# Joins of softmax statistics behind a given product's splits, layer-end tiles in a fixed order, the recurrence's Ln and Exp grouped and its large products off POOL

## The chip, the cores and the metric

The kernel runs on one core of one Trainium2 chip. The metric is the device time of one execution in microseconds (us), the median of several executions. A core has five engines that run side by side and meet only through semaphores: PE (TensorE, matrix products), DVE (VectorE), ACT (ScalarE, functions from tables), POOL (GpSimd) and SP (SyncE), which here issues almost all transfers. Each engine takes its own instructions in the order in which they were written for it.

## The reference, cut to what matters

The reference is two layers of one kind and two of another, on one sequence of 512 tokens with 1024 features. The first block is

```python
for layer in range(2):
    h = rms_norm(x, norm_mix_pre[layer])
    h = dilated_attention_mixer(h, ...) if layer % 2 == 0 else rglru_mixer(h, ...)
    x = x + rms_norm(h, norm_mix_post[layer])
    h = conv_ffn(rms_norm(x, norm_ffn_pre[layer]), ...)
    x = x + rms_norm(h, norm_ffn_post[layer])
```

The attention has eight heads of width 128 and two groups, one on neighbouring tokens and one on every fourth token. Each group gives an output and a log-sum, and the two are joined by a softmax over the groups:

```python
mx = jnp.max(logits, axis=-1, keepdims=True); p = jnp.exp(logits - mx)
s = jnp.sum(p, axis=-1, keepdims=True)
o = jnp.einsum('...qk,...kd->...qd', p, v) / s;  lse = mx + jnp.log(s)
alpha = jax.nn.softmax(jnp.stack(lses), axis=0)
o = jnp.sum(alpha[..., None] * jnp.stack(outs), axis=0)
```

The recurrence of the second layer (LRU) is `h[t] = a[t] h[t-1] + b[t]` with `a = exp(log_a)` and `b = sqrt(1 - a^2) * i * xb`, its output multiplied by `gelu(gate)` and by a weight matrix. `conv_ffn` is an up product, a short causal convolution, `gelu(g) * v` and a down product. The second block (two layers of three attentions with gates and a merge) isn't touched by the change in its own code, but it uses `normed`, which is.

## The kernel before, in words

**Products.** Every product is taken in three matmuls of hi and lo parts (`mm3`, L40 to L47): hi by hi, hi by lo, lo by hi. A weight unit (`wunit`) is loaded by SP into a `ws` buffer of 512 KB, ACT makes its hi part `wh` (L195), DVE, or POOL where it is asked to, the lo part `wl` (L196). `split` does the same for activations. `fms` runs a product with the features as rows, `tm` with tokens as rows: four tiles of 128 tokens by 512 columns each, kept in four PSUM banks, where `tail` says how many of the last steps are done tile by tile, so that the tiles end one after another.

**Order.** The program is written out, and then a scheduler with a simulated timeline sets the order on each engine. Three things bind it: the data, `keep_in_program_order`, which pins an instruction behind everything that was written for its engine before it, and `tc.issue_after`, which sets it behind a given instruction.

**The attention** (`DilatedHead`, `dilated_attention`). Each head has three qkv products for each of two groups and, for every second head, the values. `scores` takes two orders of tokens (order 1 is the strided one), makes min and sum per row (the buffer `W`, by the accumulators of L99 on DVE and L101 on ACT), writes the probabilities into `PA` and `PB`, and sends its half of `W` to DRAM (`dx`, L102) and the other order's half back (`W` from `dx`, L103), since the two orders lay the tokens out differently. `normalize` waits for `W`, joins the statistics (L113 to L120: min, difference, Exp on ACT, product, sum, reciprocal, product, all on the small tile `c`), and scales `PA` and `PB` on POOL (L124, eight instructions). `values` transposes `PA` on PE (L134), splits into `ptA`, multiplies with the values into the only `pv` bank (L45 to L47), copies into `oT`; then the same with `PB` (L145, `ptB`, L153 and L154), where DVE adds two halves into `oT` (L157) and so frees the bank. `NORMALIZE_AFTER` and `VALUES_AFTER` say behind how many of the next head's products `normalize` and `values` are written. L113 is pinned by `keep_in_program_order`.

**The layer's end** (`post_and_next`, `advance`, `normed`, `turned`). The mixer's last product `tm` gives token tiles in two column halves (`y0`, `y1`); each is squared and multiplied by a gain, its reciprocal root-mean-square is made (`rstd2`, a small power on POOL, L347), x is updated (L396), the next norm taken (`normed`, L302 to L309: two squares of 512 columns on ACT, `rstd2`, then one column half on DVE, L309, and the other on ACT and POOL, L306 and L307) and the tile turned on PE (L317).

**The recurrence** (`lru_layer`). `front` does the input product, the convolution (L571, L573) and the gates (L713); `recur` takes four of eight feature tiles at a time: Exp, Tanh, a clamp (L721 to L723), Ln and Exp (L728, L729), then L733 to L740 on DVE but for `y*v`, which is on POOL (L734). The last loop multiplies by the Gelu gate on POOL (L759). The input product's units from the second group of columns on have their lo part made on POOL.

Of the kernel before, what the change touches and what calls it, by code (L numbers as in the profile page):

```python
# [18 lines left out]
D = 1024  # L19
# [11 lines left out]
NORMALIZE_AFTER, VALUES_AFTER = 5, 7  # L31
# [11 lines left out]
def mm3(nc, out, lh, ll, rh, rl, start, stop):  # L43

    nc.tensor.matmul(out, lh, rh, start=start, stop=False)  # L45
    nc.tensor.matmul(out, lh, rl, start=False, stop=False)  # L46
    nc.tensor.matmul(out, ll, rh, start=False, stop=stop)  # L47


class DilatedHead:  # L50
# [54 lines left out]
    def normalize(self):  # L105
# [6 lines left out]

        n.tc.keep_in_program_order(nc.vector.tensor_tensor(r, nm[:, :, 0], nm[:, :, 1], op=OP.min))  # L113
# [46 lines left out]
class Net:  # L160
    def __init__(self, ctx, tc, ins, out):
# [16 lines left out]
        self.junk = self.vp.tile([128, 512], mybir.dt.bfloat16, name="junk")  # L178
# [12 lines left out]
    def split(self, hi, lo, src, eng=None, scale=None):  # L191

        nc = self.nc
        if scale is None:
            nc.scalar.copy(hi, src)  # L195
            (eng or nc.vector).tensor_tensor(lo, src, hi.bitcast(F32), op=OP.subtract)  # L196
        else:
            nc.scalar.mul(hi, src, scale)
            nc.vector.scalar_tensor_tensor(lo, src, scale, hi.bitcast(F32), op0=OP.mult, op1=OP.subtract)

    def wunit(self, src, eng=None):
# [6 lines left out]
        self.split(wh, wl, ws, eng)  # L208
# [6 lines left out]
    def fms(self, w, cols, rh, rl, n=128, kt=KD, group=1, eng=None):  # L215
# [19 lines left out]
    def tm(self, w, col, n, lh, ll, kt=KD, banks=0, tail=0, hold=None):  # L235
# [8 lines left out]
        us = []  # L244
        for k0 in range(0, kt, a):
# [5 lines left out]
            for ks in (ks[:-1], ks[-1:]) if hold and k0 + a == kt else (ks,):  # L251
                if hold and ks[-1] == kt - 1:
                    hold()
                for t in range(NT):
                    for k in ks:
                        mm3(nc, ps[t][:, :n], lh(k, t), ll(k, t), wh[:, k - k0], wl[:, k - k0], k == 0, k == kt - 1)
# [39 lines left out]
    def normed(self, xt, g, xn):  # L296

        nc = self.nc
        ss = self.stat(2)
        halves = (slice(0, 512), slice(512, 1024))  # L300
        for c, cs in enumerate(halves):
            nc.scalar.activation(xn[c], xt[:, cs], AF.Square, accum_out=ss[:, c:c + 1])  # L302
        r = self.rstd2(ss[:, 0:1], ss[:, 1:2])
        for c, cs in enumerate(halves):
            if c:
                nc.scalar.mul(xn[c], xt[:, cs], r)  # L306
                nc.gpsimd.tensor_tensor(xn[c], xn[c], g[:, cs], op=OP.mult)  # L307
            else:
# [1198 lines left out]
```

## Time and profile before

| | us |
|---|---|
| median of 3 executions | 2910.41 (2906.74 to 2910.72) |
| the profiled execution | 2905.02 |
| its span, first to last instruction | 2903.2 |
| PE busy / DVE / ACT / POOL | 2781.5 / 1641.1 / 1302.4 / 666.1 |
| mean granted TensorE clock | 0.983 of full speed |

The profiled execution is one of its own, 5.4 us below the median of the others, and 1.8 us of it lie outside the span. A PE that is busy 96% of the span can be made faster only where it isn't busy, and where it is busy at the lower of its two clocks (1.2 and 2.4 GHz; a granted clock of 0.5 in the records is the lower). In time the attention lies at 13 to 629 us of the span, the first FFN at 629 to 1009, the recurrence at 1009 to 1200, the second FFN at 1200 to 1625, the second block's layers at 1625 to 2275 and 2275 to 2903.

### The profile page before, as it was taken

To read this page: it belongs to the slowest core of one execution; us is meant where nothing else is said; L and a number is where in the kernel's file an instruction comes from. 1 tells how busy PE (TensorE), PEld (TensorE's weight loads), DVE (VectorE), ACT (ScalarE), POOL (GpSimd) and SP (SyncE) were. 2 spreads that over 40 slices of the span, in tenths; PEclk is the share of its full clock that TensorE was granted. 3 is DMA by queue.
4 is the path that set the end of the run, shared out by engine and by line. 5 is a ranking of instruction groups with operands and counts; after the bars stand their busy time and mean duration, and the time that the engine had idled before them with its cause. 6 is when DMAs were issued, how large, how long until landed. Compare 5 with 4: busy or idle time off the path is not lost.

```text
span 2903.2 us, 40547 instructions
## 1 busy us (share of the span) xinstructions
PE 2781.5 (96%) x15005; PEld 2381.3 (82%) x15005; DVE 1641.1 (57%) x3245; ACT 1302.4 (45%) x2570; POOL 666.1 (23%) x771
## 2 busy tenths in 40 slices
PE   8998898889999997999999999999999999999999
PEld 6887777778888885888888898888988898888987
DVE  4235443465552458655533767767654767767653
ACT  3233333354442355444422654665543554665542
POOL 1001110121110125211100343333421343343420
PEclk9999999899999998999999999999999999999999
DMA  5553332243333332433332524113234524113233
GB/s 176 167 159 84 88 97 64 74 130 97 100 107 111 111 122 73 134 99 94 99 127 94 152 69 107 54 50 82 63 88 130 150 66 113 47 50 82 63 98 106
DMA packets 392253, 288.60 MB, mean 99 GB/s; under 512 B 33608, under 2 KB 351816, under 8 KB 392056
## 3 DMA queue, kind: packets, MB, share of 16 engines
q1 hardware_dynamic: 382928, 268.94, 31.8%
q10 hardware_dynamic: 9128, 17.07, 1.6%
q8 instruction: 119, 1.95, 0.3%
q14 instruction: 78, 0.64, 0.1%
HBM read 266.86 MB, written 21.20 MB: 99 GB/s over the span
## 4 chain that ended last, share of the span: by engine, by line
PE 81%; DVE 7%; DMA 5%; issue 3%; ACT 3%; POOL 2%; SPq 0%; DVEq 0%; ACTq 0%; POOLq 0%
PE acc L45 20%; PE acc L46 20%; PE acc L47 20%; PE tr L843 3%; PE pv L903 2%; PE sc L46 2%; PE sc L45 2%; PE sc L47 2%; DMA dx<-W 2%; PE tr L45 1%; DVE wl L196 1%; PE tr L47 1%; PE tr L46 1%; PE pv L47 1%; PE pv L46 1%
## 5 line engine op out<-in xcount | busy, mean ns | idle before, releaser
L196 DVE TENSOR_TENSOR wl<-ws,wh 128x1024 fp32r<-128x1024 f32 (+5 forms) x463 | 550.8, 1190 | 649.5 <-ACT wh L195 645.8
L195 ACT CAST wh<-ws 128x1024 fp32r<-128x1024 f32 (+2 forms) x476 | 469.4, 987 | 754.1 <-PE acc L46 292.0
L45 PE MATMUL acc<-hH,wh 128*128 128x512 f32 (+1 forms) x1928 | 748.0, 389 | 16.9 <-DVE gate L750 8.0
L47 PE MATMUL acc<-hH,wl 128*128 128x512 f32 (+1 forms) x1928 | 744.5, 387 | 2.0 <-POOL wl L196 2.0
L46 PE MATMUL acc<-hL,wh 128*128 128x512 f32 (+1 forms) x1928 | 744.2, 386 | 1.6 <-DVE hL L196 1.4
L45 PEld LDWEIGHTS acc<-hH,wh 128*128 128x128 f32 x1928 | 366.5, 191 | 87.4 <-issue 10.0
L47 PEld LDWEIGHTS acc<-hH,wl 128*128 128x128 f32 x1928 | 367.2, 190 | 72.2 <-POOL wl L196 3.6
L46 PEld LDWEIGHTS acc<-hL,wh 128*128 128x128 f32 x1928 | 367.3, 191 | 69.3 <-DVE hL L196 2.6
L46 PE MATMUL acc<-wl,hH 128*128 128x256 f32 (+3 forms) x928 | 277.4, 300 | 0.9 <-DVE wl L196 0.7
L45 PE MATMUL acc<-wh,hH 128*128 128x256 f32 (+3 forms) x928 | 275.6, 299 | 2.0 <-ACT hH L195 1.5
L47 PE MATMUL acc<-wh,hL 128*128 128x256 f32 (+3 forms) x928 | 274.9, 299 | 0.0
L45 PEld LDWEIGHTS acc<-wh,hH 128*128 128x128 f32 x928 | 177.7, 192 | 8.2 <-ACT hH L195 2.0
L46 PEld LDWEIGHTS acc<-wl,hH 128*128 128x128 f32 x928 | 177.8, 192 | 7.3 <-DVE wl L196 1.8
L47 PEld LDWEIGHTS acc<-wh,hL 128*128 128x128 f32 x928 | 177.7, 192 | 4.3 <-DVE hL L196 0.4
L636 POOL TENSOR_TENSOR cv<-cv 128x512 f32<-128x512 f32 x48 | 62.0, 1291 | 463.0 <-DVE cv L573 449.3
L573 DVE SCALAR_TENSOR_TENSOR cv<-acc,cw,cv 128x511 f32<-128x511 f32 (+1 forms) x192 | 142.5, 746 | 3.2
L124 POOL TENSOR_SCALAR PA<-PA,c 128x256 f32<-128x256 f32 (+1 forms) x32 | 22.0, 704 | 494.2 <-DVE c L120 257.5
L876 ACT ACTIVATE P<-P,soft 128x128 f32<-128x128 f32 (+1 forms) x192 | 108.1, 563 | 60.8 <-DVE soft L875 56.6
L806 POOL TENSOR_TENSOR hst<-hst,mhalf 128x4 f32<-128x4 f32 (+2 forms) x90 | 91.6, 1022 | 175.4 <-DVE hst L805 171.4
L843 PE MATMUL tr<-ident,P 128*128 128x128 f32 x720 | 123.8, 275 | 4.1 <-POOL P L1278 2.2
L875 DVE CUSTOM_DVE_ANT_0 P<-sc,causal 128x128 f32<-128x128 f32 (+1 forms) x192 | 93.1, 485 | 52.7 <-PE tr L843 34.6
L878 POOL TENSOR_SCALAR P<-P,soft,ngate 128x128 f32<-128x128 f32 (+3 forms) x128 | 87.0, 684 | 140.2 <-DVE soft L877 128.8
(464 smaller groups left out, 5159.3 us busy)
## 6 DMA issues: line engine op xcount, KB each, us to landing
ws<-in_w_in_dram SPq DMA_DIRECT2D x116, 512.0 KB
ws<-in_ffn_w_up_dram SPq DMA_DIRECT2D x96, 512.0 KB
ws<-in_attn_w_qkv_dram SPq DMA_DIRECT2D x72, 512.0 KB
ws<-in_ffn_w_down_dram SPq DMA_DIRECT2D x48, 512.0 KB
x<-x ACTq DMA_DIRECT2D x16, 512.0 KB
ws<-in_lru_w_in_dram SPq DMA_DIRECT2D x16, 512.0 KB
ws<-in_w_mem_kv_dram SPq DMA_DIRECT2D x16, 512.0 KB
ws<-in_w_out_dram SPq DMA_DIRECT2D x16, 512.0 KB
```

Source lines behind the costliest of these rows:

```text
L45: nc.tensor.matmul(out, lh, rh, start=start, stop=False)
L46: nc.tensor.matmul(out, lh, rl, start=False, stop=False)
L47: nc.tensor.matmul(out, ll, rh, start=False, stop=stop)
L195: nc.scalar.copy(hi, src)
L196: (eng or nc.vector).tensor_tensor(lo, src, hi.bitcast(F32), op=OP.subtract)
L573: nc.vector.scalar_tensor_tensor(dst[:, s:], ps[:, :T - s], cw(taps - 1 - s), dst[:, s:], op0=OP.mult, op1=OP.add)
L636: nc.gpsimd.tensor_tensor(g, g, v, op=OP.mult)
L806: nc.gpsimd.tensor_tensor(st[:, 1], st[:, 0], self.mhalf[:rows, :nh], op=OP.pow)
L843: self.nc.tensor.transpose(ps[:, a * 128:(a + 1) * 128], s, self.ident)
L875: nc.vector.tensor_tensor_reduce(out=P, in0=S, in1=self.causal[:, 512 - n:512], scale=-1.0, scalar=BIG, op0=OP.add, op1=OP.min, accum_out=m)
L876: nc.scalar.activation(P, P, AF.Exp, bias=m, scale=-1.0, accum_out=s)
L878: nc.gpsimd.tensor_scalar(P, P, r, mult, op0=OP.mult, op1=OP.mult)
```

## The change

Six edits, which need not go together:

1. The attention's min (L113 before, L122 after) is no longer pinned in program order; it is set behind the hi and lo splits of the product that was written just before it (`done`, with `behind`). `VALUES_AFTER` goes from 7 to 6, so `values` follows one product earlier. For the last head, whose joins are made in the out product's `hold`, the joins go behind the last splits of `oT` and of the weight unit.
2. `tm` chains the token tiles of its tail: a tile's tail follows the tile before it, by `issue_after`, and the first tile's tail follows the last matmul ahead of it. After the attention, `y1` as a whole follows the last matmul of `y0`.
3. `normed` takes one square of 1024 columns and one reciprocal root, and makes both column halves on DVE. ACT's product and POOL's product go.
4. In the recurrence, `Ln` of four tiles stands ahead of `Exp` of four tiles by `issue_after`; before, the two were written tile by tile.
5. In the recurrence, `y*v` and `hs*g` go from POOL to DVE.
6. The lo parts of the recurrence's input weights go from POOL to DVE (`eng` is gone from `fms` and `wunit`).

```diff
-NORMALIZE_AFTER, VALUES_AFTER = 5, 7
+NORMALIZE_AFTER, VALUES_AFTER = 5, 6
...
+@contextmanager
+def behind(tc, *ins):
+
+    with ExitStack() as st:
+        for i in ins:
+            if i is not None:
+                st.enter_context(tc.issue_after(i.ins))
+        yield
...
-        n.tc.keep_in_program_order(nc.vector.tensor_tensor(r, nm[:, :, 0], nm[:, :, 1], op=OP.min))
+        nc.vector.tensor_tensor(r, nm[:, :, 0], nm[:, :, 1], op=OP.min)
...
-            us = [self.wunit(wv[:, :, c:c + n], eng if q else None) for c in g]
+            us = [self.wunit(wv[:, :, c:c + n]) for c in g]
...
         for t in range(NT):
-            for k in range(last, kt):
-                wh, wl = us[k // a]
-                mm3(nc, ps[t][:, :n], lh(k, t), ll(k, t), wh[:, k % a], wl[:, k % a], k == 0, k == kt - 1)
+            with behind(self.tc, end):
+                for k in range(last, kt):
+                    wh, wl = us[k // a]
+                    end = mm3(nc, ps[t][:, :n], lh(k, t), ll(k, t), wh[:, k % a], wl[:, k % a], k == 0, k == kt - 1)
+            self.last_pe = end
             yield ps[t]
...
-        ss = self.stat(2)
-        halves = (slice(0, 512), slice(512, 1024))
-        for c, cs in enumerate(halves):
-            nc.scalar.activation(xn[c], xt[:, cs], AF.Square, accum_out=ss[:, c:c + 1])
-        r = self.rstd2(ss[:, 0:1], ss[:, 1:2])
-        for c, cs in enumerate(halves):
-            if c:
-                nc.scalar.mul(xn[c], xt[:, cs], r)
-                nc.gpsimd.tensor_tensor(xn[c], xn[c], g[:, cs], op=OP.mult)
-            else:
-                nc.vector.scalar_tensor_tensor(xn[c], xt[:, cs], r, g[:, cs], op0=OP.mult, op1=OP.mult)
+        ss = self.stat()
+        nc.scalar.activation(xn[2] if len(xn) > 2 else self.junk, xt, AF.Square, accum_out=ss)
+        r = self.rstd(ss, 128, 1.0 / D)
+        for c, cs in enumerate((slice(0, 512), slice(512, 1024))):
+            nc.vector.scalar_tensor_tensor(xn[c], xt[:, cs], r, g[:, cs], op0=OP.mult, op1=OP.mult)
...
-        y1 = self.tm(w, 512, 512, lh, ll, kt=kt, banks=3 if hold else 1, tail=4)
+        y1 = self.tm(w, 512, 512, lh, ll, kt=kt, banks=3 if hold else 1, tail=4, after=self.last_pe if hold else None)
...
+        def normalize(a):
+
+            with behind(self.tc, *done):
+                a.normalize()
...
-                    self.split(v4[:, 0], v4[:, 1], ps, scale=None if u else 128 ** -0.5)
+                    done[:] = self.split(v4[:, 0], v4[:, 1], ps, scale=None if u else 128 ** -0.5)
...
-                last()
+                last((*done, *self.last_split))
...
-        return self.fms(self.i["lru_w_in"][0], self.lru_cols(), *h, group=3, eng=self.nc.gpsimd)
+        return self.fms(self.i["lru_w_in"][0], self.lru_cols(), *h, group=3)
...
-                        nc.scalar.activation(ys[-1], th[2 * m], AF.Ln, bias=tiny)
-                        last = nc.scalar.activation(ys[-1], ys[-1], AF.Exp, scale=-0.5)
+                        last = nc.scalar.activation(ys[-1], th[2 * m], AF.Ln, bias=tiny)
+                with self.tc.issue_after(last.ins):
+                    for y in ys:
+                        last = nc.scalar.activation(y, y, AF.Exp, scale=-0.5)
...
-                    nc.gpsimd.tensor_tensor(y, y, v, op=OP.mult)
+                    nc.vector.tensor_tensor(y, y, v, op=OP.mult)
...
-                nc.gpsimd.tensor_tensor(hs[m], hs[m], g, op=OP.mult)
+                nc.vector.tensor_tensor(hs[m], hs[m], g, op=OP.mult)
```

The change shifts lines: L113 becomes L122, L157 becomes L166, L196 becomes L204, L199 L206, L733 to L740 become L744 to L751, and L750 becomes L761.

On DVE in the attention, at the end of the second head's scores, the order before is this (`ptB` is the lo split of the head before, `c` the joins, `oT` the additions that free the `pv` bank, `wl` and `qk` the splits of the next products):

```order
L196 TENSOR_TENSOR ptB<-tr,ptB 128x512
L113 TENSOR_TENSOR c<-W 128x2x4
L115 TENSOR_TENSOR c<-c,W 128x2x4 x2
L196 TENSOR_TENSOR wl<-ws,wh 128x1024
L157 TENSOR_TENSOR oT<-oT,pv 128x2x128
L199 SCALAR_TENSOR_TENSOR qk<-acc,qk 128x512
L117 TENSOR_TENSOR c<-c,W 128x4x4
L157 TENSOR_TENSOR oT<-oT,pv 128x2x128
L118 TENSOR_TENSOR c<-c 128x2x4
```

and in the changed kernel, at the same place, behind the two `ptB` splits and the last accumulators of the scores:

```order
L204 TENSOR_TENSOR wl<-ws,wh 128x1024
L204 TENSOR_TENSOR qk<-acc,qk 128x512
L166 TENSOR_TENSOR oT<-oT,pv 128x2x128 x2
L204 TENSOR_TENSOR wl<-ws,wh 128x1024
L206 SCALAR_TENSOR_TENSOR qk<-acc,qk 128x512
L166 TENSOR_TENSOR oT<-oT,pv 128x2x128 x2
L204 TENSOR_TENSOR vL<-v,vH 128x1024 x2
L204 TENSOR_TENSOR wl<-ws,wh 128x1024
L204 TENSOR_TENSOR qk<-acc,qk 128x512
L122 TENSOR_TENSOR c<-W 128x2x4
L124 TENSOR_TENSOR c<-c,W 128x2x4 x2
```

The join has moved behind three weight splits, three product splits and all four additions into `oT`, which before stood behind it.

On DVE in the first half of the recurrence (`th` and `y` are its tiles, `xl` the convolution's lo split, `gate` a copy that frees an `acc` bank) the order before is

```order
L733 TENSOR_TENSOR th<-th,y 128x512
L750 COPY gate<-acc 128x512
L735 SCALAR_TENSOR_TENSOR th<-y,th 128x512
L196 TENSOR_TENSOR xl_7324<-xb,xh_7323 128x512
L733 TENSOR_TENSOR th<-th,y 128x512
L738 SCALAR_TENSOR_TENSOR th<-a,th 128x512
```

and in the changed kernel

```order
L761 COPY gate<-acc 128x512
L744 TENSOR_TENSOR th<-th,y 128x512
L745 TENSOR_TENSOR y<-y,th 128x512
L744 TENSOR_TENSOR th<-th,y 128x512 x2
L204 TENSOR_TENSOR wl<-ws,wh 128x1024
L745 TENSOR_TENSOR y<-y,th 128x512
L204 TENSOR_TENSOR xl_7276<-xb,xh_7275 128x512
L746 SCALAR_TENSOR_TENSOR th<-y,th 128x512
```

The products `y*v` (L745) and the weights' `wl` now stand in DVE's row; before, they were on POOL.

## Rows read from the trace of the kernel before

**Rows 1.** Page, part 1: busy us (share of the span), instructions

```profile
PE 2781.5 (96%) x15005; PEld 2381.3 (82%) x15005; DVE 1641.1 (57%) x3245; ACT 1302.4 (45%) x2570; POOL 666.1 (23%) x771
```

**Rows 2.** PE's waits, whole span: line <- releaser: us, times, longest

```profile
PE pv L153 <- DVE c L118: 26.9, 5, 5.8
...
PE acc L45 <- ACT hH L195: 7.0, 7, 2.5
...
PE pv L153 <- DVE c L119: 6.1, 1, 6.1
```

**Rows 3.** Timeline of PE: start, us, instruction [idle before it <- releaser]

```profile
264.31 0.55 PE L153 MATMUL pv<-ptB,vH 128*128 128x256 f32 x1 [5.53 <-DVE c L118]
...
596.39 1.97 PE L317 MATMUL acc<-ident,spare 128*128 128x128 f32 x8 [6.84 <-DVE spare L309]
```

**Rows 4.** Timeline of DVE, a head in the middle and the last head

```profile
246.54 0.69 DVE L196 TENSOR_TENSOR ptB<-tr,ptB 128x512 fp32r<-128x512 f32 x1
260.86 0.17 DVE L113 TENSOR_TENSOR c<-W 128x8 f32<-128x8 f32 x1 [13.64 <-issue]
...
261.23 1.22 DVE L196 TENSOR_TENSOR wl<-ws,wh 128x1024 fp32r<-128x1024 f32 x1
...
264.50 0.17 DVE L120 TENSOR_TENSOR c<-c 128x8 f32<-128x8 f32 x1
...
550.68 0.17 DVE L113 TENSOR_TENSOR c<-W 128x8 f32<-128x8 f32 x1 [10.34 <-DMA W<-dx]
...
552.06 0.17 DVE L120 TENSOR_TENSOR c<-c 128x8 f32<-128x8 f32 x1
```

**Rows 5.** Timeline of SP's queue in the same head

```profile
247.29 0.37 SPq L102 DMA_DIRECT2D dx<-W  x1
258.98 0.36 SPq L103 DMA_DIRECT2D W<-dx  x1
```

**Rows 6.** Stretches: us, busy us per engine, PEclk, DMA share, GB/s

```profile
247.00:258.00 11.00, 11.00 (x54) 9.25 (x53) 0.23 (x1) 1.80 (x4) 0.00 (x0) 1.00 0.19 39
258.00:268.00 10.00, 4.47 (x17) 3.65 (x16) 6.66 (x15) 1.63 (x3) 3.16 (x6) 0.75 0.28 77
...
241.00:541.00 300.00, 267.01 (x1328) 227.11 (x1328) 136.28 (x301) 110.09 (x224) 32.40 (x48) 0.93 0.30 81
...
1078.00:1124.00 46.00, 32.96 (x125) 24.38 (x124) 41.24 (x42) 29.14 (x41) 22.49 (x10) 0.89 0.28 84
1124.00:1163.00 39.00, 32.65 (x128) 25.60 (x127) 32.22 (x28) 19.68 (x29) 20.70 (x12) 0.87 0.26 86
```

**Rows 7.** POOL's scaling of the probabilities: ns min/median/max, and one head

```profile
L124 POOL TENSOR_SCALAR PA<-PA,c x32: 374/475/2443, 221.3 to 555.7; 128x256 f32<-128x256 f32 x24, 128x128 f32<-128x128 f32 x8
...
264.84 2.60 POOL L124 TENSOR_SCALAR PA<-PA,c 128x128 f32<-128x128 f32 x4 [38.91 <-DVE c L120]
```

**Rows 8.** POOL's groups at 1009 to 1203: count, busy us, mean ns, idle before

```profile
L196 POOL TENSOR_TENSOR wl<-ws,wh 128x1024 fp32r<-128x1024 f32 x13 | 33.1, 2550 | 67.5 <-ACT wh L195 67.5
L759 POOL TENSOR_TENSOR th<-th,gate 128x512 f32<-128x512 f32 x8 | 13.7, 1721 | 16.1 <-DVE th L740 16.1
L734 POOL TENSOR_TENSOR y<-y,th 128x512 f32<-128x512 f32 x8 | 13.6, 1720 | 7.1 <-DVE th L733 7.1
L307 POOL TENSOR_TENSOR spare<-spare,gb 128x512 f32<-128x512 f32 x5 | 6.6, 1315 | 3.0 <-ACT spare L306 3.0
```

**Rows 9.** Timeline of DVE in the recurrence's first half, and one instruction of POOL

```profile
1089.18 1.29 DVE L733 TENSOR_TENSOR th<-th,y 128x512 f32<-128x512 f32 x2 [1.02 <-ACT y L729]
...
1098.26 2.88 DVE L738 SCALAR_TENSOR_TENSOR th<-a,th 128x512 f32<-128x512 f32 x1
...
1103.94 0.68 DVE L738 SCALAR_TENSOR_TENSOR th<-a,th 128x512 f32<-128x512 f32 x1
...
1119.23 0.68 DVE L750 COPY gate<-acc 128x512 f32<-128x512 f32 x1
...
1097.74 2.84 POOL L196 TENSOR_TENSOR wl<-ws,wh 128x1024 fp32r<-128x1024 f32 x1
```

More of the change, by code (lines that the diff above doesn't have):

```diff
@@ L1 @@
 import itertools
-from contextlib import ExitStack
+from contextlib import ExitStack, contextmanager
 import numpy as np
@@ L46, in mm3 @@
     nc.tensor.matmul(out, lh, rl, start=False, stop=False)
-    nc.tensor.matmul(out, ll, rh, start=False, stop=stop)
+    return nc.tensor.matmul(out, ll, rh, start=False, stop=stop)
+@contextmanager
[5 more added lines that the diff above has]
+        yield
 class DilatedHead:
@@ L177, in __init__ @@
         self.vp = self.vctx.enter_context(tc.tile_pool(name="vecs", bufs=1))
-        self.junk = self.vp.tile([128, 512], mybir.dt.bfloat16, name="junk")
+        self.junk = self.vp.tile([128, D], mybir.dt.bfloat16, name="junk")
     def bank(self, tag="acc"):
@@ L194, in split, with wunit @@
         if scale is None:
[L195 to L201 removed]
+            return nc.scalar.copy(hi, src), (eng or nc.vector).tensor_tensor(lo, src, hi.bitcast(F32), op=OP.subtract)
+        return (nc.scalar.mul(hi, src, scale),
+                nc.vector.scalar_tensor_tensor(lo, src, scale, hi.bitcast(F32), op0=OP.mult, op1=OP.subtract))
+    def wunit(self, src):
         nc = self.nc
@@ L207, in wunit @@
         wl = self.wp.tile(shape, F32R, tag="wl", bufs=SEC_BUFS["w"], name="wl")
-        self.split(wh, wl, ws, eng)
+        self.last_split = self.split(wh, wl, ws)
         return wh, wl
@@ L213, in fm, with fms @@
         return next(self.fms(w, [col], rh, rl, n, kt))
-    def fms(self, w, cols, rh, rl, n=128, kt=KD, group=1, eng=None):
+    def fms(self, w, cols, rh, rl, n=128, kt=KD, group=1):
         nc = self.nc
@@ L233, in fms, with tm @@
             q += len(g)
-    def tm(self, w, col, n, lh, ll, kt=KD, banks=0, tail=0, hold=None):
+    def tm(self, w, col, n, lh, ll, kt=KD, banks=0, tail=0, hold=None, after=None):
         nc = self.nc
@@ L243, in tm @@
         last = kt - a * tail
-        us = []
+        us, end = [], after
         for k0 in range(0, kt, a):
@@ L458, in dilated_attention @@
         vectors = self.vectors()
-        later, vs = [], {}
+        later, vs, done = [], {}, []
         n = 0
@@ L501, in dilated_attention @@
             if hd < 7:
-                after(NORMALIZE_AFTER, a.normalize)
+                after(NORMALIZE_AFTER, normalize, a)
                 after(VALUES_AFTER, values, a)
@@ L505, in dilated_attention, with last @@
         due(True)
-        def last():
-            a.normalize()
+        def last(ins):
+            done[:] = ins
+            normalize(a)
             values(a)
@@ L546, in attn_layer @@
             for k in range(KD - 1):
-                self.split(oh[0][:, k], oh[1][:, k], oT[:, k])
+                done = self.split(oh[0][:, k], oh[1][:, k], oT[:, k])
             def hold():
-                last()
+                last((*done, *self.last_split))
                 self.split(oh[0][:, KD - 1], oh[1][:, KD - 1], oT[:, KD - 1])
@@ L1365, in memory @@
             nc.sync.dma_start(mt, i["mem_2"][0, t * 128:(t + 1) * 128])
-            rows.append(self.normed(mt, gm, (xn[:, :512], xn[:, 512:])))
+            rows.append(self.normed(mt, gm, (xn[:, :512], xn[:, 512:], xn)))
         Q = [self.state([128, 2, 2, T]) for _ in range(2)]
```

7 lines of the change are left out of this document (3 added, 4 removed).

## The prediction

> **What bounds the kernel now.** I began with the page's busy shares: PE works 96% of the span [rows 1], so the end is set by PE, and only two things can be gained: the time in which PE stands, and the time in which it works at the lower clock. The list of PE's waits comes next. Its longest entry is one place in the attention, the first product with `ptB` (L153), six times behind the joins `c`, 26.9 + 6.1 = 33.0 us [rows 2]. The stretch 241 to 541, which holds six heads, says the same: 300 us, PE busy 267.0, so 33.0 idle, at a mean granted clock of 0.93 [rows 6]. Two other places stand out: the layer's end after the attention, where PE waits 6.84 us for the normed tile [rows 3], and the recurrence, where PE is busy 32.96 of 46 and 32.65 of 39 us at clocks of 0.89 and 0.87 [rows 6], 19.4 us idle.
>
> The cause in the attention is read on DVE. `ptB` is split at 246.54; the next instruction is the pinned min, and it starts at 260.86, after 13.6 us in which DVE does nothing [rows 4]. It waits for `W`: SP sends `dx` at 247.29 and can only ask for `W` at 258.98 [rows 5]. Behind the min stand the weights' `wl` and the additions into `oT` that free the one `pv` bank. PE has products ready until 258.8, then stands until 264.31 [rows 3], and comes back at half speed: in 258 to 268 the mean clock is 0.75, five of ten microseconds at the lower level [rows 6], while in 247 to 258, when it was busy throughout, the clock was 1.00 [rows 6].
>
> **The joins (edit 1).** The order of the changed kernel puts three weight splits, three product splits and the four additions ahead of the min. All that these need is PE, ACT and earlier loads, so DVE works through the 13.6 us, `pv` comes free, and PE isn't stopped at L153. What is late next? The first transposes of the new `PA`. By the order, PE has about 98 matmuls of 128x512 besides small ones between the last scores and these. In 247 to 258 it does 54 records in 11.0 us [rows 6], nearly all of that form, and a few records may be missing, so I take 0.23 us each: about 23 us, some 24 with the small ones. Counted from the scores' end near 245.4, as `ptB` is split just after it, PE asks for `PA` near 269. `W` was there at 260.86 [rows 4]. The joins take 552.06 + 0.17 - 550.68 = 1.55 us where nothing stands between them, and 3.8 us in the middle head, with other work between [rows 4]. The first `PA` tile took 0.4 to 1.24 us on POOL, and four took 2.60 [rows 7]. So the first two tiles are ready between 263.1 and 266.3, 3 to 6 us before PE asks. The whole wait goes: 33.0 us. The lower clock goes with it: 0.07 of 300 us is 21 us if PE had worked through all of it; in 258 to 268, PE works from 264.31 on, 3.7 of the five slow microseconds, a share of 0.74, so 21 x 0.74 = 16 us. Together **49 us**. DVE's own load (136 us busy in 300) and SP's loads (DMA share 0.30) [rows 6] leave room for a head that is 8 us shorter. I leave out the last head: its joins too stand behind more work, but `y1` may no longer fill PE's wait for them; both sides are a few microseconds, so 0, bounded by -5 and +5.
>
> **The layer's end after the attention (edits 2 and 3).** The tiles now end one after another, some 5 us apart (24 matmuls of 0.23 us), so the chain of square, root, x, square, root and product is hidden behind the next tile for three of four. The 6.84 us [rows 3] go, with about half as much for the clock (16 for 33 in the heads), 3 us. Against it stands the last tile, whose chain nothing hides except the first products of the FFN; I give back 3. **7 us**, bounded by 0 and 10. At the other layer ends PE's waits for `hH` come to 7.0 us in seven places [rows 2]; a shorter `normed` (no 1.3 us product on POOL [rows 8], one square for two) and ordered tiles should save a part: **3 us**, bounded by 0 and 7.
>
> **The recurrence (edits 4 to 6).** POOL loses 13 weight splits of 2.55 us, 8 of 1.72 and 8 of 1.72 [rows 8]. DVE takes them. A weight split costs DVE 1.22 us with POOL at rest [rows 4]; a two-operand product of 128x512 on DVE is nearest to the 0.68 us row at 1103.94 [rows 9]. The bill is 13 x 1.22 + 16 x 0.68 = 26.7 us more DVE work. But DVE's own operations were stretched: the same L738 takes 0.68 us alone and 2.88 us at 1098.26, when POOL ran a weight split of 2.84 us from 1097.74 [rows 9]. The lock on memory that this looks like is paid by DVE: 2.2 us for one POOL instruction. The place that stopped PE longest here is the third gate copy, at 1119.23, 30 us after the first L733 at 1089.18 [rows 9]. In the changed order 16 operations of about 0.68 us and one weight split stand between them: 16 x 0.68 + 1.2 = 12 us. So the copy is some 17 us earlier and PE isn't stopped. PE's idle 19.4 us and its slow clock (0.11 x 46 + 0.13 x 39 = 10 us at the most, 7 with the share above) make 26 us that can be had. DVE was busy 41.2 of 46 and 32.2 of 39 us [rows 6] and will be the next bound: with the stretching gone and the new work added, I expect stretches of about 38 and 34 us, with PE's own work at 30 or less. That gives 13 us, and up to 3 more where `hs*g` leaves POOL: **16 us**, bounded by 0 and 24. The grouping of Ln and Exp (edit 4) I cost at nothing: ACT isn't what DVE or PE mostly waits for there.
>
> The Trainium skill, "SBUF — State Buffer", section "Who interferes with whom", calls the port pair of DVE and GpSimd an exclusive lock: a DVE instruction with two SBUF inputs and a GpSimd instruction that reads SBUF don't overlap, and the later one stands until the first has ended. By that rule the move takes away all of the stretching, which the row at 1098.26 bears out; but it also says that POOL's scaling of `PA` will now meet a DVE that never rests, and that is the first rival's condition.
>
> **The rest.** The start of the program gains about 1 us, since `normed` no longer waits on POOL. New small waits I put at 4 us (DVE's row is denser). Sum: 49 + 7 + 3 + 16 + 1 - 4 = 72 us. From the profiled execution, 2905.0 - 72 = 2833.0; the median of before was 5.4 us above that execution, so the prediction for the median is 2838.4, said as **2838**. A difference of 0.2%, 6 us, is about what a measurement of this kernel can tell from none.
>
> **The rivals.** *First, the joins are late at the next place.* PE is in order, so if `PA` isn't ready it stops at L134. The margin is 3 to 6 us. POOL's scaling took 0.475 us in the middle and 2.44 at the most [rows 7]; if a weight split of 1.22 us gets ahead of each of four tiles, they end 4 x 1.2 = 4.9 us later, and if the min too waits its turn behind splits of 1.2 to 2.4 us, the margin is used up by 1 to 4 us in each of seven heads. Three us a head with half again for the clock is some 30 us: 2868. For it: DVE's row is full there. Against it: PE needs only two of four tiles at first, and the median scaling was unhindered. Chance 0.15. By the rule of the Trainium skill named above it would be this and no more, since the lock is held for one instruction at a time.
>
> *Second, the recurrence is bound by DVE.* The 26.7 us of new work are not paid by less stretching, and PE waits for DVE as long as before: the 16 us fall away, 2854. For it: 41.2 of 46 us busy already. Against it: the 2.88 beside 0.68. Chance 0.13.
>
> *Third, slower than before.* The attention's round trip of `W` becomes longer: it took 11.7 us while PE stood still for half of it and SP loaded little (DMA share 0.19 and 39 GB/s in 247 to 258 [rows 6]). With a PE that never rests, loads of weights lie in that stretch. Each microsecond over the margin of 3 to 6 us is one of PE's, and half again for the clock, in seven heads. To eat 72 us it needs 72 / (7 x 1.5) = 7 us beyond the margin, a trip of 22 to 25 us instead of 11.7; with two more, 2926. Nothing in the trace shows such a trip, so 0.03.
>
> *Fourth, it doesn't do what it says.* PE's stop at L153 is not DVE's but another wait's, and the six stops stay: 49 us less, 2887. The releaser named is `c`, and `oT` stands right behind it in the order, so 0.04.
>
> **How the numbers follow.** Forecast 0.65, with its own range 2822 to 2852 from the bounds above; rivals 0.15, 0.13, 0.03 and 0.04. The range 2812 to 2876 takes in the first two and some more on the lower side, since the bounds of the smaller terms reach 25 us below the forecast together. Faster by over 0.2% are all but the third and a part of nothing else: 0.95; within 0.2%: 0.02; slower: 0.03.
>
> **What would show it.** In the profile after: no wait of PE at the `ptB` products and no DVE gap of 13 us ahead of the min, with a clock near 1.00 in 241 to 500; the heads' period from 49 to about 40.5 us; L738's mean at 0.68 us; no gate copy among PE's releasers. A list of waits with `tr` behind POOL's `PA` several times would mean the first rival, one with `acc` behind DVE's `wl` in the recurrence the second.

## The result and the profile after

The changed kernel takes 2834.47 us (2831.17 to 2835.07, four executions) against 2908.57 us for the kernel before, a ratio of 0.9747 with a 95% interval of 0.9728 to 0.9765. That is 74 us less by the medians; the forecast was 2838 us, and its range held the time. The profiled execution has a span of 2832.7 us, 70.5 us less, at a mean granted clock of 0.992 instead of 0.983.

Page, part 1, of the changed kernel, which answers to [rows 1]:

```profile
PE 2759.5 (97%) x15005; PEld 2367.8 (84%) x15005; DVE 1640.2 (58%) x3274; ACT 1278.1 (45%) x2486; POOL 552.2 (19%) x714
```

PE's busy time fell by 22 us with the same 15005 matmuls: that is the part of the gain that is clock, and the rest of the 70.5 us, some 48, is time in which PE stood. POOL lost 114 us, and yet DVE's sum stayed, 1641.1 to 1640.2, though it took 29 instructions more: what POOL had done to DVE's operations was worth about as much as the work that moved. The 40 operations of the recurrence that stayed on DVE (L733, L735 and L737 to L739) took 50.4 us before and 27.0 in the changed kernel.

Both kernels run the same number of matmuls, so the stretch between the starts of two matmuls of the same number compares their stages (us, from the two profiled executions):

| stretch, by number of the matmul | before | after | difference | forecast |
|---|---|---|---|---|
| start to the first head's scores (0 to 842) | 190.9 | 194.2 | +3.3 | -1 |
| heads (842 to 2310) | 332.7 | 284.9 | -47.8 | -49 |
| last head, out product, layer end (to 2700) | 90.7 | 86.0 | -4.6 | -7 |
| first FFN and its end (to 4600) | 418.4 | 416.1 | -2.3 | -3 for all layer ends |
| recurrence (to 5200) | 162.6 | 144.3 | -18.3 | -16 |
| second FFN and its end (to 7400) | 448.9 | 450.1 | +1.2 | in the -3 |
| second block (to 15003) | 1241.8 | 1240.2 | -1.6 | in the -3 |

(The forecast had +4 for small new waits besides.) How far a stretch of one trace can be trusted is shown by the kernels below that leave it as it was: the start took 190.9 us in all five of them, the heads 328.3 to 333.0, the stretch with the last head 90.5 to 92.2, the first FFN 418.0 to 418.8, the second FFN 448.5 to 450.1, the second block 1240.9 to 1244.2. The recurrence took 162.6 to 163.4. So the first five differences stand clear of that spread, and the last two don't, or hardly.

PE's waits over the whole span of the changed kernel, which answer to [rows 2] (line <- releaser: us, times, longest):

```profile
PE acc L320 <- DVE xn L312: 12.5, 1, 12.5
PE acc L320 <- DVE o L312: 7.7, 2, 4.3
PE tr L143 <- POOL PA L133: 7.2, 1, 7.2
PE acc L45 <- ACT gate L769: 6.4, 1, 6.4
PE acc L45 <- ACT hH L204: 5.3, 5, 2.1
...
PE pv L162 <- DVE oT L166: 1.4, 1, 1.4
```

The first line is the program's start (12.7 us before). The second stands where the two layers of the second block begin, and PE waited as long there before, 6.9 us for `st` and 0.8 for `o`. The 33 us at the products with `ptB` are gone but for 1.4 us in the last head. `PA` is waited for once, in the last head too. Of the recurrence's list one long entry is left, and it is ACT's.

In the heads themselves (columns as in [rows 6]):

```profile
231.00:480.00 249.00, 247.28 (x1295) 210.30 (x1294) 135.32 (x293) 105.44 (x217) 27.43 (x48) 1.00 0.42 97
480.00:560.00 80.00, 65.16 (x315) 54.61 (x315) 43.81 (x88) 31.48 (x65) 8.30 (x15) 0.88 0.31 92
```

PE stands for 1.7 of 249 us, and the granted clock is 1.00 where it was 0.93. The 80 us around the last head and the layer's end have 14.8 us of waits and a clock of 0.88.

DVE in a head of the changed kernel, which answers to [rows 4]:

```profile
254.25 1.23 DVE L204 TENSOR_TENSOR wl<-ws,wh 128x1024 fp32r<-128x1024 f32 x1 [0.60 <-ACT wh L204]
255.40 0.68 DVE L206 SCALAR_TENSOR_TENSOR qk<-acc,qk 128x512 fp32r<-128x512 f32 x1
263.71 1.23 DVE L204 TENSOR_TENSOR wl<-ws,wh 128x1024 fp32r<-128x1024 f32 x1 [7.63 <-ACT wh L204]
264.85 0.68 DVE L204 TENSOR_TENSOR qk<-acc,qk 128x512 fp32r<-128x512 f32 x1
265.45 0.16 DVE L122 TENSOR_TENSOR c<-W 128x8 f32<-128x8 f32 x1
...
266.82 0.17 DVE L129 TENSOR_TENSOR c<-c 128x8 f32<-128x8 f32 x1
```

The min doesn't wait any more: it starts as its turn comes, right behind the third product's split. It is so in six of the eight heads; in the first it waits 2.5 us for `W`, in the last 3.5. DVE still rests, 7.6 us, but behind a weight that isn't there yet and that PE doesn't need yet. The transfers on SP's queue, as in [rows 5]:

```profile
248.33 0.36 SPq L112 DMA_DIRECT2D dx<-W  x1
259.42 0.36 SPq L113 DMA_DIRECT2D W<-dx  x1
```

and POOL's scaling with the transposes that need it:

```profile
267.16 2.80 POOL L133 TENSOR_SCALAR PA<-PA,c 128x128 f32<-128x128 f32 x4 [38.06 <-ACT wh L204]
...
270.75 0.93 PE L143 MATMUL tr<-ident,PA 128*128 128x128 f32 x7
```

The scaling begins 3.6 us ahead of the transposes and its four tiles are ready 0.8 us ahead. In the next heads the distance from the scaling's start is 3.6 us again (308.13 to 311.76, 349.80 to 353.38, and so in all six).

### The profile page after: what moved, and what is told of

It reads as the page before. It is cut to its first block, busy times and chain, and to the rows that moved or that the text cites. A ratio compares the mean times of both kernels' runs of the same rounds, so it can differ in the third digit from the quotient of the medians.

```text
span 2832.7 us, 40391 instructions
## 1 busy us (share of the span) xinstructions
PE 2759.5 (97%) x15005; PEld 2367.8 (84%) x15005; DVE 1640.2 (58%) x3274; ACT 1278.1 (45%) x2486; POOL 552.2 (19%) x714
## 4 chain that ended last, share of the span: by engine, by line
PE 86%; DVE 6%; DMA 4%; ACT 3%; issue 1%; POOL 1%; SPq 0%; ACTq 0%; DVEq 0%; POOLq 0%
PE acc L46 21%; PE acc L45 21%; PE acc L47 21%; PE tr L854 3%; PE pv L914 2%; PE sc L45 2%; PE sc L47 2%; PE sc L46 2%; PE tr L45 2%; PE tr L47 2%; PE tr L46 2%; DVE wl L204 1%; PE pv L46 1%; PE pv L47 1%; PE pv L45 1%
## 5 line engine op out<-in xcount | busy, mean ns | idle before, releaser
L204 DVE TENSOR_TENSOR wl<-ws,wh 128x1024 fp32r<-128x1024 f32 (+2 forms) x476 | 563.5, 1185 | 679.2 <-ACT wh L204 666.8
L204 ACT CAST wh<-ws 128x1024 fp32r<-128x1024 f32 (+2 forms) x476 | 469.7, 987 | 781.7 <-PE acc L46 275.5
L204 DVE TENSOR_TENSOR pt<-tr,pt 128x128 fp32r<-128x128 f32 (+2 forms) x224 | 104.0, 474 | 22.7 <-ACT pt L204 21.7
```

The lines of the kernel that those rows point to most:

```text
L204: return nc.scalar.copy(hi, src), (eng or nc.vector).tensor_tensor(lo, src, hi.bitcast(F32), op=OP.subtract)
```

## The experiments

The theory was the prediction's: each edit gains at its own place, the joins most, since DVE's row no longer holds the splits behind a transfer. Kernels whose names begin with b are the kernel before with one part of the change, those with a the changed kernel with one part undone or moved. All compute the whole reference.

### The joins alone, and all but the joins

`b_join` is the kernel before with edit 1 whole:

```diff
-NORMALIZE_AFTER, VALUES_AFTER = 5, 7
+NORMALIZE_AFTER, VALUES_AFTER = 5, 6
...
-        n.tc.keep_in_program_order(nc.vector.tensor_tensor(r, nm[:, :, 0], nm[:, :, 1], op=OP.min))
+        nc.vector.tensor_tensor(r, nm[:, :, 0], nm[:, :, 1], op=OP.min)
...
+            with behind(self.tc, *done):
+                a.normalize()
```

> The kernel before with the joins alone moved (edit 1 with VALUES_AFTER 6 and the last head's part; tiles, norm and recurrence as before). Theory: the six stops of PE at the ptB products and their slow clock go as in the changed kernel, so the stretch from the first head's scores to the last head's shrinks from 333 to about 285 us; with the last head, whose wait for PA has more products ahead of it in this order, the whole is 48 to 54 us faster, 2855 to 2861 us. Rival (the stops belong to another wait, or the joins come late at the transposes of PA): under 30 us faster, 2880 us or more.

Measured: 2854.67 us against 2905.59, a ratio of 0.9823 (0.9806 to 0.9840), 51 us. The heads took 288.1 us, 44.6 less than before; the last head and the layer's end 3.8 less.

`a_pin` is the changed kernel with the joins put back:

```diff
-NORMALIZE_AFTER, VALUES_AFTER = 5, 6
+NORMALIZE_AFTER, VALUES_AFTER = 5, 7
...
-        nc.vector.tensor_tensor(r, nm[:, :, 0], nm[:, :, 1], op=OP.min)
+        n.tc.keep_in_program_order(nc.vector.tensor_tensor(r, nm[:, :, 0], nm[:, :, 1], op=OP.min))
...
-            with behind(self.tc, *done):
-                a.normalize()
+            a.normalize()
```

> The changed kernel with the joins put back: the min is pinned in program order and VALUES_AFTER is 7; all else stays changed. Theory: DVE stands for some 13 us ahead of the min in each head again and PE 5.5 us at the ptB products, so 47 to 52 us slower than the changed kernel, 2881 to 2886 us, and the gain that is left, about 25 us, is that of the other edits. Rival (the edits overlap, and a recurrence or layer end without stops would have been gained anyway by the joins): the difference is below 40 us.

Measured: 2878.71 us, a ratio to before of 0.9908 (0.9891 to 0.9925). That is 44 us above the changed kernel's median, 3 less than the least expected and over the rival's 40; with each taken against the kernel before of its own set of runs (26.9 and 74.1 us below it) it is 47. The heads took 330.0 us. The same 200 us of the attention in `a_pin` and then in the changed kernel:

```profile
240.00:440.00 200.00, 179.49 (x894) 152.62 (x893) 92.27 (x203) 74.76 (x152) 21.61 (x32) 0.94 0.33 88
```

```profile
240.00:440.00 200.00, 199.42 (x1036) 169.26 (x1035) 107.10 (x234) 81.72 (x168) 22.85 (x40) 1.00 0.43 100
```

With the pin PE stands for 20.5 of 200 us and does 894 matmuls; without it 0.6 us and 1036. Taken from both sides, edit 1 is worth 44 to 51 us. `VALUES_AFTER` changes in both kernels with the min's place; it wasn't run by itself, but the next kernel keeps it at 6.

### Is it enough to take the pin away?

`a_free` takes away the edge behind the product's splits and leaves the min to the scheduler:

```diff
-            with behind(self.tc, *done):
-                a.normalize()
+            a.normalize()
```

> The changed kernel without the order ahead of the min: neither pinned nor set behind a product's splits, so the scheduler puts it behind the first product instead of the third, where W is still 8 us away. Theory: place is all that counts, so DVE stands some 8 us again, with the second product's weight split behind the min, and PE runs out of split weights for 1 to 3 us a head: 10 to 30 us slower than the changed kernel, 2844 to 2864 us. Rival (taking the pin away is enough, since PE has weights ahead): no change, 2832 to 2837 us.

Measured: 2879.54 us, a ratio to before of 0.9908 (0.9891 to 0.9924), 45 us above the changed kernel. The direction was the theory's and the size was not: nothing is left of the gain in the heads (330.7 us). DVE shows why:

```profile
251.76 0.68 DVE L204 TENSOR_TENSOR qk<-acc,qk 128x512 fp32r<-128x512 f32 x1
267.00 0.17 DVE L122 TENSOR_TENSOR c<-W 128x8 f32<-128x8 f32 x1 [14.56 <-issue]
```

The scheduler set the min behind one product's split only, and DVE stood there for 14.6 us, as long as with the pin (13.6, [rows 4]). I had counted on 8 us. In its stretch 231 to 480, PE was busy 225.41 of 249 us at a clock of 0.92. So the gain isn't in taking away the pin, nor in `VALUES_AFTER`, but in saying where the min belongs; the place that the scheduler chose is too early.

### How much room is there behind it?

`a_late` writes the joins one product later:

```diff
-NORMALIZE_AFTER, VALUES_AFTER = 5, 6
+NORMALIZE_AFTER, VALUES_AFTER = 6, 6
```

> The changed kernel with the joins one product later (NORMALIZE_AFTER 6 instead of 5), so behind a fourth product's splits; the order puts the PA transposes 2.3 us of PE's work later too. Theory: the joins are set by DVE's order and not by W any more; their scaling begins 3.6 us ahead of the transposes in the changed kernel, so some 6 us later and with 2.3 us back PE waits 0 to 1.5 us in each of six or seven heads, with the slow clock 0 to 14 us in all, 2834 to 2848 us. Rival (the joins wait for W anyway, so the order doesn't matter): no change at all, and the min waits for its transfer.

Measured: 2830.95 us (2830.51 to 2831.34), a ratio to before of 0.9740 (0.9725 to 0.9754). No loss, and neither theory nor rival in its working: the min waits for nothing here in any head, so `W` isn't the bound, and yet nothing was lost by the later place. Its rows (stretch, then POOL and PE):

```profile
231.00:480.00 249.00, 249.00 (x1315) 213.54 (x1314) 138.32 (x303) 109.28 (x221) 31.17 (x53) 1.00 0.36 97
```

```profile
269.14 1.73 POOL L133 TENSOR_SCALAR PA<-PA,c 128x128 f32<-128x128 f32 x4 [35.19 <-ACT PB L111]
...
273.32 0.50 PE L143 MATMUL tr<-ident,PA 128*128 128x128 f32 x3
```

The scaling began only 2.0 us later in time than in the changed kernel, not 6, and the transposes 2.6 us later, so the distance grew to 4.2 us. Counted from `dx` (248.33 there, 249.52 here) the min even starts at the same distance, 17.1 us: in the changed kernel DVE stood for 7.6 us ahead of the third product's weight split, and the fourth product found room in such time. So one more product ahead of the join didn't cost the join that product's time. PE stands nowhere in these 249 us. The kernel is 3.5 us below the changed one by the medians, and its heads took 281.4 us, against 284.9 to 285.9 in three kernels with the changed kernel's place (the changed one, `a_start` and `a_y1free`); but the two weren't run side by side and their intervals overlap, so I don't call it faster than that one, only faster than before.

### The recurrence

`b_pool` is the kernel before with edits 5 and 6:

```diff
-                    nc.gpsimd.tensor_tensor(y, y, v, op=OP.mult)
+                    nc.vector.tensor_tensor(y, y, v, op=OP.mult)
...
-                nc.gpsimd.tensor_tensor(hs[m], hs[m], g, op=OP.mult)
+                nc.vector.tensor_tensor(hs[m], hs[m], g, op=OP.mult)
...
-        return self.fms(self.i["lru_w_in"][0], self.lru_cols(), *h, group=3, eng=self.nc.gpsimd)
+        return self.fms(self.i["lru_w_in"][0], self.lru_cols(), *h, group=3)
```

> The kernel before with the large products of the recurrence taken off POOL alone (edits 5 and 6: y*v, hs*g and the lo parts of its input weights on DVE). Theory: DVE's own operations lose the 1.1 to 2.2 us by which POOL stretched them, and that pays for the 27 us of new work, so the recurrence's 191 us shrink by 13 to 18: 2891 to 2896 us. Rival (DVE is the bound there and the new work isn't paid): no gain or a loss, 2906 to 2916 us.

Measured: 2904.34 us against 2907.26, a ratio of 0.9991 (0.9982 to 1.0001). The interval takes in no gain at all, so the theory's 13 to 18 us fall; 2.9 us by the medians is nearest to the rival, but the rival's mechanism isn't what the trace shows. DVE's operations did lose their stretching, as the L738 group at 1020 to 1130 shows (0.68 us beside 2.88 in [rows 9]):

```profile
L738 DVE SCALAR_TENSOR_TENSOR th<-a,th 128x512 f32<-128x512 f32 x4 | 2.7, 676 | 0.0
```

What ate the gain, as the two kernels with the edge below bear out, is on ACT, in groups at 1010 to 1130 of `b_pool`:

```profile
L728 ACT ACT_TABLE_LOAD x6 | 7.7, 1283 | 0.1
L729 ACT ACT_TABLE_LOAD x6 | 7.7, 1283 | 0.1
```

With another work on DVE the scheduler no longer grouped Ln and Exp by itself, and ACT loaded tables 12 times for them instead of four, eight times 1.28 us more, 10.3 us. Its PE then waited 11.3 us for the gate:

```profile
PE acc L45 <- ACT gate L758: 11.3, 1, 11.3
```

`b_pool6` moves the weights' lo parts alone, and leaves `y*v` and `hs*g` on POOL:

```diff
-        return self.fms(self.i["lru_w_in"][0], self.lru_cols(), *h, group=3, eng=self.nc.gpsimd)
+        return self.fms(self.i["lru_w_in"][0], self.lru_cols(), *h, group=3)
```

> The kernel before with only the lo parts of the recurrence's input weights moved from POOL to DVE (edit 6). Theory: these are 33 of POOL's 60 us there and the longest single instructions (2.5 us), so they do most of the stretching: 7 to 13 us faster, 2896 to 2902 us, with y*v still at 1.7 us on POOL. Rival (the products y*v in the chain are what counts): under 4 us.

Measured: 2899.72 us, a ratio of 0.9975 (0.9965 to 0.9985), 7.5 us: at the lower end of what was expected, and by the medians 4.6 us better than moving all of it, though the two intervals touch. It loads eight tables for Ln and Exp, four fewer than `b_pool`.

`b_lnexp` is the edge alone:

```diff
-                        nc.scalar.activation(ys[-1], th[2 * m], AF.Ln, bias=tiny)
-                        last = nc.scalar.activation(ys[-1], ys[-1], AF.Exp, scale=-0.5)
+                        last = nc.scalar.activation(ys[-1], th[2 * m], AF.Ln, bias=tiny)
+                with self.tc.issue_after(last.ins):
+                    for y in ys:
+                        last = nc.scalar.activation(y, y, AF.Exp, scale=-0.5)
```

> The kernel before with Ln grouped ahead of Exp in the recurrence alone (edit 4). Theory: the scheduler had grouped them already, ACT loads as many tables as before, and ACT isn't waited for: within 2 us of the kernel before. Rival (the chain of Ln, table, Exp is on the path): 3 us or more either way.

Measured: a ratio of 0.9998 (0.9989 to 1.0007). Alone it does nothing, as expected: the order was so already. `b_lru` puts it together with the two edits of `b_pool`; its diff is those two.

> The kernel before with the whole of the recurrence's edits (4, 5 and 6: Ln ahead of Exp by an edge, and its large products off POOL). Without the edge, edits 5 and 6 moved the DVE work so that the scheduler alternated Ln and Exp, with 12 table loads instead of 4 of 1.28 us, and gained 3 us of the 16 that I had put down to them. Theory: the edge isn't worth nothing but 8 of 16 us or more once POOL is left, and the three edits together give what the changed kernel shows in the recurrence: 4 table loads of Ln and Exp and 15 to 19 us, 2888 to 2892 us. Rival (the gain of the recurrence needs the ordered tiles or the norm too): 3 to 8 us, 2899 to 2904 us.

Measured: 2891.86 us against 2906.00, a ratio of 0.9953 (0.9937 to 0.9970), 14 us, and in the matmuls 4600 to 5000, where the changed kernel is 18.1 us shorter than before, 17.4 us. Against `b_pool`, from which only the edge sets it apart, the matmuls 4600 to 5200 took 149.0 instead of 161.1 us, and PE stood there for 12.6 instead of 22.8. It is back at four loads:

```profile
L728 ACT ACT_TABLE_LOAD x2 | 2.6, 1283 | 0.0
L731 ACT ACT_TABLE_LOAD x2 | 2.6, 1283 | 0.0
```

In the end of the layer it loses 3.7 us, where the changed kernel, with the new norm and the ordered tiles, loses nothing; which of the two does that wasn't tested. So the three edits belong together: edits 5 and 6 gave 3 us and the edge 1, neither told from nothing by its interval, and all three 14. The edge is what keeps the others' gain. The Trainium skill, "ScalarE: Activation LUTs", section "What ACT_TABLE_LOAD costs", gives about 1283 ns for the load itself; the rows agree to the nanosecond. It adds a drain of about 1.4 us for each switch to a different set; the traces don't show one: in the changed kernel a load starts at 1037.47, 0.02 us behind the end of the `Ln` ahead of it, and the `Exp` starts 0.02 us behind the load's end. The measurement decides here: 1.28 us for a switch.

### The norm, the tiles and the program's start

`b_normed` is the kernel before with the new `normed` and what it needs:

```diff
+        ss = self.stat()
+        nc.scalar.activation(xn[2] if len(xn) > 2 else self.junk, xt, AF.Square, accum_out=ss)
+        r = self.rstd(ss, 128, 1.0 / D)
+        for c, cs in enumerate((slice(0, 512), slice(512, 1024))):
+            nc.vector.scalar_tensor_tensor(xn[c], xt[:, cs], r, g[:, cs], op0=OP.mult, op1=OP.mult)
```

> The kernel before with the norm alone changed (edit 3: one square of 1024 columns, one root, both halves on DVE). Theory: the layer ends gain 3 to 5 us together and the program's start loses about 3, since DVE makes all eight halves ahead of the weight splits and PE then waits for the third weight unit: 2903 to 2910 us. Rival (the norm carries the gain at the layer end after the attention): 7 us or more faster.

Measured: 2904.74 us against 2907.26, 0.9991 (0.9982 to 1.0001). The time is where it was expected, and isn't told from no change; the reasons aren't: the start didn't lose 3 us but gained 1.7, and the stretches with layer ends are 2 us longer together in its trace, not 3 to 5 shorter.

`b_tiles` is the kernel before with the tiles in order:

```diff
+            with behind(self.tc, end):
+                for k in range(last, kt):
+                    wh, wl = us[k // a]
+                    end = mm3(nc, ps[t][:, :n], lh(k, t), ll(k, t), wh[:, k % a], wl[:, k % a], k == 0, k == kt - 1)
...
+        y1 = self.tm(w, 512, 512, lh, ll, kt=kt, banks=3 if hold else 1, tail=4, after=self.last_pe if hold else None)
```

> The kernel before with the token tiles of a layer's end in a fixed order alone (edit 2). Theory: the wait of 6.8 us for the normed tile after the attention goes with its slow clock, some 7 us, and 1 or 2 us at the other layer ends, but the last head's wait for PA has no y1 product to fill it: 4 to 9 us faster, 2899 to 2904 us. Rival (the norm is what counts there): under 3 us.

Measured: 2903.09 us, 0.9987 (0.9978 to 0.9996), 4 us faster. The layer's end after the attention gained 2.9 us, the first FFN 1.6, and the start lost 3.4. (In its trace the heads took 4.4 us less too, where nothing was changed; that is the spread told of above.) That is the loss of the changed kernel at its start. PE in `b_tiles` there:

```profile
22.61 0.50 PE L46 MATMUL acc<-wl,hH 128*128 128x512 f32 x1 [0.82 <-DVE wl L206]
25.53 0.50 PE L46 MATMUL acc<-wl,hH 128*128 128x512 f32 x1 [0.83 <-DVE wl L206]
27.47 0.49 PE L45 MATMUL acc<-wh,hH 128*128 128x512 f32 x1 [0.52 <-ACT wh L205]
28.73 0.50 PE L46 MATMUL acc<-wl,hH 128*128 128x512 f32 x1 [0.77 <-DVE wl L206]
```

`a_start` had been made for the wrong suspect, the norm:

```diff
-                self.turned(self.normed(xt, gn, xn), h, t)
+                self.turned(self.normed_halves(xt, gn, xn), h, t)
```

(`normed_halves` is the old `normed`.)

> The changed kernel with the old norm (two squares, the second half on ACT and POOL) at the program's start alone. Theory: the 3.1 us that the changed kernel lost at the start (PE ahead by 2.2 us at its 40th matmul and behind by 3.1 at its 80th) come from DVE making all eight normed halves ahead of the weight splits; with the old norm they come back: 2830 to 2833 us, 2 to 4 us faster than the changed kernel. Rival (they come from the transfers of the weights): no change.

Measured: 2834.57 us, a ratio of 0.9755 (0.9742 to 0.9768), no change, and the start as long as in the changed kernel (194.4 us): that theory falls. What stands in its place, as I read the traces: the first value product is a `tm` with eight steps, two to a weight unit, and `tail=4`, so all of it is tail. With the tiles chained, the first tile wants all four weight units before the second tile may start, while they are still being loaded and split; before, PE went on with other tiles on the units that it had. The waits above are for just these splits, `b_normed` has none there, and both kernels with the edge and the old norm have them. A kernel that leaves this one product unchained wasn't run.

`a_y1free` takes away the edge that holds `y1` behind `y0` after the attention:

```diff
-        y1 = self.tm(w, 512, 512, lh, ll, kt=kt, banks=3 if hold else 1, tail=4, after=self.last_pe if hold else None)
+        y1 = self.tm(w, 512, 512, lh, ll, kt=kt, banks=3 if hold else 1, tail=4)
```

> The changed kernel without the edge that holds all of y1 behind the last matmul of y0 after the attention; its tiles stay in order among themselves. Theory: the first products of y1 that need no last head fill PE's wait of 7.2 us for PA, so 3 to 7 us faster, 2827 to 2832 us. Rival (a critical chain from the last statistics to the last oT sets this stage, and the filler only moves the wait, or the tiles end together again): within 2 us or slower.

Measured: 2833.22 us, a ratio of 0.9752 (0.9739 to 0.9765), no change; the stretch took 86.4 us, 0.4 more than in the changed kernel. That is the rival: what PE is given to do meanwhile doesn't shorten this stage. The traces say why. This is the chain that ended last, in the changed kernel (start, us, what):

```profile
495.30 9.82 DMA dx<-W
505.14 0.36 SPq L113
505.60 5.19 DMA ws<-in_attn_w_o_dram
510.86 1.05 ACT wh L204
511.94 1.23 DVE wl L204
...
514.51 2.06 PE tr L143 x7
```

SP asks for the out product's next weights only behind its request of `W`, which comes when `dx` has landed. And the joins of the last head, whose min ran at 508.52, stand behind these weights on ACT, with their Exp (L125):

```profile
510.86 1.04 ACT L204 CAST wh<-ws 128x1024 fp32r<-128x1024 f32 x1 [6.62 <-DMA ws<-in_attn_w_o_dram]
511.81 0.21 ACT L125 ACTIVATE c<-c 128x16 f32<-128x16 f32 x1
```

So they took 5.4 us, to 513.89, where 1.55 had been enough [rows 4]. In `a_y1free` the chain up to `wl` is the same (9.84, 0.36, 5.23, 1.05 and 1.24 us) and goes on into PE's first product of `y1` with these weights, for which PE waits 4.3 us: the wait moved. A kernel that asks for these weights ahead of `W` wasn't run.

## Why the prediction was right, step by step

**The total: partly luck.** 72 us were forecast, and the two traces differ by 70.5. The start came out 4.3 us worse than forecast and the stretch with the last head 2.4; what made up for them is the 4 us put aside for small new waits, which named no place, and 2.3 us more in the recurrence. The large terms are another matter.

**The joins: right, in mechanism and size.** 49 us were forecast, 47.8 measured in the changed kernel's heads, and 44 to 51 us from the two sides by themselves. The two parts of the sum are there too, in the heads' stretch before and after (columns as in [rows 6]):

```profile
203.62:536.31 332.69, 297.75 (x1471) 252.13 (x1470) 154.83 (x357) 120.67 (x247) 36.98 (x56) 0.93 0.30 81
```

```profile
206.72:491.58 284.86, 283.13 (x1471) 240.20 (x1469) 156.84 (x357) 118.96 (x247) 32.07 (x56) 1.00 0.41 95
```

PE's standing fell from 34.9 to 1.7 us, where 33 were forecast, and its busy time by 14.6 us, where 16 were forecast for the clock. One link read differently: I had the joins start when `W` lands, at 260.9 in that head's time, with 3 to 6 us to spare. In fact they start behind the third product's split in six of eight heads, and the 3.6 us to spare are the distance between two places in the order, the same in each of the six.

**The first rival, joins late at the transposes,** happened in the last head alone, where PE waited 7.2 us for `PA`. I had put this head at zero: the waits of its joins and of the last products (6.3, 1.8, 1.5 and 1.8 us before) became 2.1, 7.2, 1.4 and 2.0, 1.3 us more, so zero was about right. But the forecast had only DVE's order in view: the joins were held up by the wait for `W` (3.5 us) and, on ACT, by weights that SP asks for behind `W`.

**The layer's end after the attention:** 7 forecast. The wait of 6.84 us [rows 3] became 1.5 and 0.4 us, and the stretch with the last head lost 4.6 us. The 3 us for the clock didn't come: the granted clock in that stretch was 0.91 before and 0.88 after. The credit was put to the ordered tiles and the norm; alone the tiles gave 2.9 there, the norm nothing, and the joins alone 3.8, so the parts seem to overlap, and the split among the edits was wrong, as far as stretches with a spread of 1.7 us can tell.

**The other layer ends:** 3 forecast. The first FFN's stretch lost 2.3 us, and with the tiles alone 1.6; the later ones can't be told from no change. That the shorter norm gains at a layer end, no run shows.

**The recurrence: the size right, one step wrong.** 16 forecast, 18 measured. The stretching of DVE by POOL was real and is gone. But "the grouping of Ln and Exp I cost at nothing" held only for the order of the kernel before; with the other edits, and without the edge, eight more table loads come in, and three edits that seemed to be worth 16 us and nothing gave 3 and 1 apart, which is within the noise, and 14 together. The grouping must be costed against the order that the other edits make, not against the one in the trace. PE's stop at the gate copy of 8.0 us went, but 6.4 us at the Gelu gate came, behind the second Exp group and one more table: what was next late was ACT, which I had set aside. The second rival, a recurrence bound by DVE, didn't come: PE waited 1.8 us there for DVE's `wl`.

**The start: wrong sign.** A gain of 1 us was forecast from the norm, and the norm by itself did gain 1.7; I had overlooked that edit 2 also orders the tiles of the first value product. Edit 2 alone cost 3.4 at the start.

**The third rival,** a longer trip of `W` under a denser row of transfers, didn't come: 11.1 us from `dx` to the request of `W` in the rows above, beside 11.7 in [rows 5]. In that very stretch the transfers were hardly denser (a DMA share of 0.25 and 43 GB/s at 248 to 259, beside 0.19 and 39); but in the head at 289.28 the trip took 11.8 us at a share of 0.47, and at 371.95 it took 11.7 us at 0.53. (Its price of 2926 was counted from the profiled execution; from the forecast median, like the others, it is 2931.) **The fourth,** that the stops were not the min's, is excluded by `a_free` and `a_pin`.

## What to carry to other kernels

An engine that takes its instructions in order should be given a wait only behind all the work that others need from it meanwhile: say in which place it belongs, since neither a pin nor a scheduler's guess put it there (13.6 and 14.6 us of standing, and 45 us of the kernel). Work that leaves one engine moves the order on all others, so an order that had come about by itself, such as functions grouped by table, should be fixed by an edge in the same change. An edge on one engine doesn't order the others: in the last head the same joins stood on ACT behind a weight that SP asked for behind their own transfer. A chain of tiles that gained where results are handed on tile by tile cost 3.4 us at the start, where the weights were still arriving.

## What the runs showed of the hardware

Not expected was how little the small transfer minds its neighbours. From `dx` of order 1 to the request of `W`, the eight heads before took 8.6 to 11.7 us: 9.7 us in the last head, with next to nothing else moving, 8.6 in the first with 76 GB/s, 11.7 in the second with 28. In the changed kernel they took 9.5 to 11.8 us. The trips of the other order, with as many bytes, took 1.6 to 3.2 us before. And a DVE instruction of 0.68 us took up to 2.2 us longer while one of POOL's ran, which added up to so much that 114 us less on POOL and 29 instructions more on DVE left DVE's busy time where it was.
